# Mixer A of a two-layer diffusion trunk: rotation tables on ScalarE, and one scan over both directions

## The chip, the cores and the metric

One core of one Trainium2 chip runs the whole program in one launch. The metric is the time of one execution on the device, in microseconds (us). The comparison is between the kernel before and the kernel with the change, on the same inputs.

## The reference, cut to what matters

The reference is one inference step of a trunk of two layers over 128 context tokens and 256 latent tokens, width 1024. Layer 0 runs two mixers side by side, layer 1 two attentions; each layer ends in a gated ConvFFN. The change lies in mixer A of layer 0, a diagonal complex state space (S5) in 32 groups of 16 channels with 64 complex states each, run once forward and once backward, the two results summed:

```python
def _s5_scan(u, lam_re, lam_im, log_dt, b_re, b_im, c_re, c_im, h0_re, h0_im):
    dt = jnp.exp(log_dt)[:, None]
    mag = jnp.exp(lam_re * dt)
    ar, ai = mag * jnp.cos(lam_im * dt), mag * jnp.sin(lam_im * dt)
    ...
    _, _, hr, hi = lax.associative_scan(_cplx_combine, elems, axis=1)
    y = jnp.einsum('blgp,gcp->blgc', hr, c_re) - jnp.einsum('blgp,gcp->blgc', hi, c_im)
    return y, hr[:, -1], hi[:, -1]
...
    y_f, hr_f, hi_f = direction(uf, 0)
    y_b, hr_b, hi_b = direction(uf[:, ::-1], 1)
    y = (y_f + y_b[:, ::-1]).reshape(bsz, n, S5_WIDTH) + ...
```

Context tokens start from a zero state and their last states are outputs. Latent tokens start from given states. Mixer B is a gated DeltaNet of four heads, also in two directions, on the same input projection.

## The kernel before, in words

**Mixer A.** Four tokens are folded into one step, so a sequence has 96 steps (32 context, 64 latent) and with three extra columns for starts NCOL = 99. The 32 groups go in four octets of 8. Partitions 0 to 63 hold the 64 states of the forward direction, partitions 64 to 127 those of the backward one, in the order of the tokens. A complex recurrence is turned into two real ones by a rotation: each input is turned back by a phase that grows with the step, a real scan with the decay runs, and the result is turned forward again. For each octet:

- `s5_tables` (L436) makes the phase `ph = fh*step + fl*step` of 8 x 99 columns, rounds off whole turns twice (`sub_round`, L308: an add and subtract of a large constant, L312, then a subtraction, L313), and from it the sine `R["sn"]` and cosine `R["cs"]` on ScalarE (`sincos`, L418). VectorE does everything else: L447, L450, L451, the rounding, the fold in L422 and the decay `R["dec"]` in L455. It then makes two matrices `bt_r`, `bt_i` (L457 to L467).
- `s5_octet` (L544) multiplies the inputs `U` by `bt_r` and `bt_i` on TensorE (L559: 64 rows of inputs, 128 columns of weights, both directions in one matmul), rotates on VectorE (L563 to L565), scans the real and the imaginary part (L575 forward half, L576 backward half read from its end), rotates four products `y` (L589, L591), and sums them on TensorE into one PSUM bank `pY` of tag `sy` (L597: taps of the same step; L600: states, with both directions in the 128 rows of a matmul and an output half of 64 columns). The sum is copied out in two pieces (L602, L603), transposed twice (L606, L613) and added to the residual (L614).

`s5_taps` (L470) runs before, once for an octet, on `mm` banks.

**The order of the work.** In `layer_ab` (L1196) the setup, four `s5_taps`, `s5_tables` of octets 0 and 1 and the norm stand ahead of the projection of `u` (tags `mm` and `pj`, two banks each). Then each octet is followed in the code by the tables of the octet two ahead, a GELU and the projections of one DeltaNet head (`pj` banks; L1107, L1108, L1109 are the three matmuls of a split product, and L271 on VectorE makes the low half `wl` of a weight unit from the high half that L270 makes on ScalarE). Head 3 and the DeltaNet cores follow in a second set of PSUM banks (`ps1`, from L1236).

The order in which instructions stand on each engine is not that of the code. The class `Order` collects all instructions with their dependences, gives each a duration from fixed formulas, and lists them by longest remaining path at the time at which each could start. Its rules that matter here: a matmul on part of the columns of the array leaves TensorE free for the next instruction 20 ns later (`free[e] = s + 20`), matmuls on disjoint columns are kept together (`gangs`), a matmul that accumulates onto a region waits for the end of the one before it on that region, and a bank in rotation waits for all users of its last tile.

```python
            free[e] = s + (20 if len(held) < 4 else time)
...
                    if (w or w2) and r[0] < r2[1] and r2[0] < r[1] and r[2] < r2[3] and r2[2] < r[3]:
                        same = self.engine[j] == e and not self.dma[j]
                        self.follow(k, j, BEHIND if same and not (w2 and not w) else WAITED)
```

The engines then run their lists in order; each waits at an instruction until its data is there.

**DeltaNet core.** `state` in `gdn_core` scales a 128x128 tile `kd` by a column of `E` on VectorE (L802), four times in each of four heads, ahead of a matmul (L804).

Of the kernel before, what the change touches and what calls it, by code (L numbers as in the profile page):

```python
# [15 lines left out]
AF = mybir.ActivationFunctionType  # L16
ALU = mybir.AluOpType
# [4 lines left out]
P = 128  # L22
# [9 lines left out]
QC = 4  # L32
NCH = T // QC
NCC = NCTX // QC
NLC = NLAT // QC
NG = 32

NCOL = NCH + 3
# [3 lines left out]
MAGIC = 12582912.0  # L42
# [5 lines left out]
def _offsets(table):  # L48
# [6 lines left out]


CST_FIRST = [
    ("nidx", QC + 1), ("one", 1), ("pih", 1), ("comb", 8), ("tstep", NCOL), ("zmask", NCOL), ("ident", 128),
    ("b16", 128),
]  # L60
CST_COLS = CST_FIRST + [
# [18 lines left out]
def _consts():  # L80
    c = {}
    i = np.arange(P)
    c["ident"] = np.eye(P)
    c["ui"] = i[:, None] <= i[None, :]
    c["li"] = i[:, None] >= i[None, :]
    c["us"] = i[:, None] < i[None, :]
    c["ls"] = i[:, None] > i[None, :]
    c["nd"] = i[:, None] != i[None, :]
    for b in (16, 32, 64):
        same = (i[:, None] // b) == (i[None, :] // b)  # L90
        c[f"b{b}"] = same
        c[f"o{b}"] = ((i[:, None] // (2 * b)) == (i[None, :] // (2 * b))) & ~same
    par = np.zeros((P, 8))
    for n, b in enumerate((16, 32, 64)):
        par[:, 2 * n] = (i // b) % 2 == 0
        par[:, 2 * n + 1] = (i // b) % 2 == 1
    c["par"] = par
    c["npar"] = -par
    c["nidx"] = np.broadcast_to(np.arange(QC + 1), (P, QC + 1))
    seq = lambda n: np.concatenate([[0], np.arange(n)])  # L100
    given = lambda n: np.concatenate([[0], np.ones(n)])
    for name, f in (("tstep", seq), ("zmask", given)):
        fwd, bwd = np.concatenate([f(NCC), f(NLC), [0]]), np.concatenate([f(NLC), f(NCC), [0]])[::-1]
        c[name] = np.concatenate([np.broadcast_to(fwd, (64, NCOL)), np.broadcast_to(bwd, (64, NCOL))])
    c["ind"] = (i[:, None] % 16) == np.arange(16)[None, :]
    dinit = np.zeros((P, 2, 16))
    for p in range(P):
        dinit[p, 0, p % 16] = 1
        dinit[p, 1, 15 - p % 16] = 1
    c["dinit"] = dinit.reshape(P, 32)  # L110

    c["wm0"] = np.where(i[None, :] <= i[:, None], 0.0, -1e30)
    c["wm1"] = np.where(i[:, None] <= i[None, :], 0.0, -1e30)
    comb = np.zeros((P, 8))
    for r in range(32):
        comb[32 * (r // 8) + r % 8, r % 8] = 1
    c["comb"] = comb
    c["one"] = np.ones((P, 1))
    c["pih"] = np.full((P, 1), math.pi / 2)
    quarter = 16  # L120
    inv = 10000.0 ** (-np.arange(quarter) / quarter)
    tok = np.arange(NLAT)
    rc, rs = np.zeros((P, 2, 2, 16)), np.zeros((P, 2, 2, 16))
    for tt in range(2):
        t = tok[tt * P:(tt + 1) * P]
        for half, pos in ((0, t // 64), (1, t % 64)):
            ang = pos[:, None].astype(np.float64) * inv[None, :]
            rc[:, tt, half], rs[:, tt, half] = np.cos(ang), np.sin(ang)
    c["rcos"], c["rsin"] = rc.reshape(P, 64), rs.reshape(P, 64)
    out = np.zeros((P, NCST), np.float32)  # L130
    for name, (at, w) in CST.items():
        out[:, at:at + w] = c[name]
    return out
# [82 lines left out]
class Trunk:  # L216
# [27 lines left out]
    def t(self, pool, shape, tag, dt=F32, bufs=None):  # L244
        bufs = bufs or pool.bufs
        name = self.uid(tag)
        self.tiles[name] = (pool.name, tag, bufs, self.n)
        return pool.tile(list(shape), dt, tag=tag, name=name, bufs=bufs)
# [187 lines left out]
    def s5_tables(self, pool, tmp, o):  # L436

        nc, v, t, S = self.nc, self.nc.vector, self.t, self.S
        ident = self.c("ident")
        R = S["R"][o]  # L440
        gs = slice(8 * o, 8 * o + 8)
        sh = [P, 8, NCOL]
        step = self.c("tstep").unsqueeze(1).to_broadcast(sh)
        R["sn"] = t(pool, sh, "s5Rs", bufs=2)
        R["cs"] = t(pool, sh, "s5Rc", bufs=2)
        ph = R["cs"]
        v.tensor_mul(ph, S["fh"][:, gs].unsqueeze(2).to_broadcast(sh), step)  # L447
        self.sub_round(tmp, ph, "s5rr")
        q = t(tmp, sh, "s5rr")
        v.tensor_mul(q, S["fl"][:, gs].unsqueeze(2).to_broadcast(sh), step)  # L450
        v.tensor_add(ph, ph, q)  # L451
        self.sub_round(tmp, ph, "s5rr")
        self.sincos(R["sn"], R["cs"], ph)
        R["dec"] = t(pool, sh, "s5dec")
        v.tensor_mul(R["dec"], S["mq"][:, gs].unsqueeze(2).to_broadcast(sh),  # L455
                             self.c("zmask").unsqueeze(1).to_broadcast(sh))
        R["bt_r"] = t(pool, [P, 4, P], "s5btr", bufs=2)  # L457
        R["bt_i"] = t(pool, [P, 4, P], "s5bti", bufs=2)
        tv = t(tmp, [P, 8, 64], "s5rr")
        for key, x0, k0, x1, k1, op in (("bt_r", "br", "bar", "bi", "bsn", ALU.add),  # L460
                                        ("bt_i", "bi", "bar", "br", "bsn", ALU.subtract)):
            ba = t(tmp, [P, 8, 64], "s5tb")
            self.s5_prod(v, o, ba, S[x0], S[k0], S[x1], S[k1], op, tv)
            pt = self.bank("mod", [P, 4, P])
            for g in range(4):
                nc.tensor.transpose(pt[:, g, :], ba[:, 2 * g:2 * g + 2, :].rearrange("p g n -> p (g n)"), ident)
            nc.scalar.copy(R[key], pt)  # L467
        return R
# [75 lines left out]
    def s5_octet(self, pool, o, uT, U, R):  # L544

        nc, v, t, S = self.nc, self.nc.vector, self.t, self.S
        ident = self.c("ident")
# [6 lines left out]
        for e in range(2):  # L554
            h = slice(64 * e, 64 * e + 64)
            sr, si = self.mm(hs), self.mm(hs)
            for out, key in ((sr, "bt_r"), (si, "bt_i")):
                for q in range(4):
                    nc.tensor.matmul(out[:, q, :], R[key][h, q, :], U[h, q, :], start=True, stop=True)  # L559
            cs, sn = R["cs"][:, e::2], R["sn"][:, e::2]  # L560
            for out, x0, x1, op in ((xr[:, e::2], sr, si, ALU.add), (xi[:, e::2], si, sr, ALU.subtract)):
                tmp = t(pool, hs, "s5C", bufs=1)
                v.tensor_mul(out, x0, cs)  # L563
                v.tensor_mul(tmp, x1, sn)
                v.tensor_tensor(out, out, tmp, op)  # L565
        for x_, st in ((xr, "st_re"), (xi, "st_im")):
            nc.scalar.copy(x_[f, :, NCC + 1], self.s(st)[f, gs])
            nc.scalar.copy(x_[b, :, NCOL - 1], self.s(st)[b, gs])
        G = []
        N = 8 * NCOL  # L570
        flat = lambda ap: ap.rearrange("p g k -> p (g k)")
        for x_, name, last in ((xr, "s5gr", "last_r"), (xi, "s5gi", "last_i")):

            g_ = t(pool, [P, N + 2], name)
            v.tensor_tensor_scan(g_[f, 2:N + 2], flat(R["dec"])[f], flat(x_)[f], 0.0, ALU.mult, ALU.add)  # L575
            v.tensor_tensor_scan(g_[b, N - 1::-1], flat(R["dec"])[b, ::-1], flat(x_)[b, ::-1], 0.0, ALU.mult, ALU.add)  # L576
            g_ = g_[:, 1:N + 1].rearrange("p (g k) -> p g k", g=8)

            nc.scalar.copy(S[last][f, gs], g_[f, :, NCC + 1])
            nc.scalar.copy(S[last][b, gs], g_[b, :, 0])  # L580
            G.append(g_[:, :, 1:NCOL - 1])

        cs, sn = R["cs"][:, :, 1:NCOL - 1], R["sn"][:, :, 1:NCOL - 1]
# [7 lines left out]
                v.tensor_mul(y, x, k)  # L591
            terms.append((y, R[mat]))

        pY = self.bank("sy", [P, 4, NCH + 1])
        for q in range(4):
            for h in (f, b):
                nc.tensor.matmul(pY[h, q, :], S["tp"][h, 4 * o + q, :], U[h, q, 1:NCOL - 1], start=True, stop=False)  # L597
            for n, (y, mat) in enumerate(terms):
                for e, h in enumerate((f, b)):
                    nc.tensor.matmul(pY[h, q, :], mat[:, 2 * q + e, :], y[:, 2 * q + e, :], start=False, stop=n == 3)  # L600
        ys = t(pool, [P, 4, NCH], "gth", bufs=2)
        nc.scalar.copy(ys[:, :, 0:NCC], pY[:, :, 0:NCC])  # L602
        nc.scalar.copy(ys[:, :, NCC:], pY[:, :, NCC + 1:])  # L603
        pt = self.bank("su", [NCH, 4, P])
        for q in range(4):
            nc.tensor.transpose(pt[:, q, :], ys[:, q, :], ident)  # L606
# [102 lines left out]
    def gdn_core(self, pool, h, kT, qT, vT, zs):  # L709
# [89 lines left out]
        def state(d, c):  # L799
            col = 4 * d + h  # L800
            kd = t(pool, [P, P], "gkd", bufs=2)
            v.tensor_scalar(kd, kh[:, c, :], E[:, 1, c, col:col + 1], None, ALU.mult)  # L802
            p1 = self.bank("g4", [P, P])
            nc.tensor.matmul(p1, kd, vn[:, d, c, :], start=True, stop=True)  # L804
            if c == 0:
                nc.scalar.copy(gnew[:, d, :], p1)
            else:
                v.scalar_tensor_tensor(S1[d], S0[d], E[:, 2, c, col:col + 1], p1, ALU.mult, ALU.add)
# [1114 lines left out]
```

## Time and profile before

| what | value |
|---|---|
| median of 3 runs | 1194.18 us (1192.45 to 1199.54) |
| profiled execution, its own time | 1194.85 us |
| its span in the trace | 1193.1 us |
| TensorE busy | 1133.0 us (95%) |
| VectorE busy | 859.4 us (72%) |
| ScalarE busy | 543.7 us (46%) |
| chain that ended last | PE 85%, DVE 10%, ACT 2% |

PE is TensorE's matmuls, PEld its weight loads, DVE is VectorE, ACT is ScalarE. The span runs from the first to the last instruction; 1.75 us lie around it. Busy shares are averages over stages that differ: the start, the octets of mixer A, the DeltaNet cores, and from about 400 us on the rest.

### The profile page before, as it was taken

Reading aid. Unit: us, or ns where it says so; the run is one execution under the profiler, and the core shown is the slowest. Engines: PE = TensorE matmul, PEld = TensorE weight load, DVE = VectorE, ACT = ScalarE, POOL = GpSimd, SP = SyncE. Lnnn points to the kernel's source line nnn. Section 1 sums busy time; section 2 is a strip of 40 time slices with the busy share of each in tenths; the row PEclk is TensorE's granted clock in tenths of the full one; section 3 lists DMA queues with packets and bytes.
Section 4 is the critical chain, followed back from the end, with each engine's and each line's share of the span. In section 5 each row is a group of like instructions: output and inputs, shape, how many; then the busy total and the mean of one; then the engine's idle time right before and its main releaser. Section 6 shows DMA issues by size and latency. Waiting matters only on the chain.

```text
span 1193.1 us, 19445 instructions
## 1 busy us (share of the span) xinstructions
PE 1133.0 (95%) x7315; PEld 980.1 (82%) x7315; DVE 859.4 (72%) x2137; ACT 543.7 (46%) x1178; POOL 2.9 (0%) x15
## 2 busy tenths in 40 slices
PE   4699999999999999999999979999998999999998
PEld 1386676687558999999999968657688999999998
DVE  8997888889878768676763458886867877766432
ACT  3442333276445546555542324554535655554221
POOL 0000000000000000000000000000000000000000
PEclk8688898999999999999999989999999999999999
DMA  9233165364884333343334432311113334333541
GB/s 378 106 111 141 54 212 187 144 227 169 306 322 129 111 106 107 124 138 111 124 113 143 124 119 91 115 52 66 36 54 106 107 123 141 110 121 105 165 134 56
DMA packets 50734, 160.80 MB, mean 135 GB/s; under 512 B 8272, under 2 KB 12240, under 8 KB 50384
## 3 DMA queue, kind: packets, MB, share of 16 engines
q1 hardware_dynamic: 49200, 154.72, 38.8%
q10 hardware_dynamic: 1440, 4.85, 1.1%
q8 instruction: 57, 0.93, 0.3%
q14 instruction: 37, 0.30, 0.1%
HBM read 156.53 MB, written 3.01 MB: 134 GB/s over the span
## 4 chain that ended last, share of the span: by engine, by line
PE 85%; DVE 10%; ACT 2%; DMA 1%; issue 1%; ACTq 0%; DVEq 0%
PE mm L1107 16%; PE mm L1108 16%; PE mm L1109 16%; PE mod L992 2%; PE mm L1343 2%; PE mm L1344 2%; PE mm L1345 2%; PE sy L600 2%; PE sc L1465 1%; PE pj L1108 1%; PE pj L1107 1%; PE mm L559 1%; PE pj L1109 1%; DVE wl L271 1%; PE mod L1107 1%
## 5 line engine op out<-in xcount | busy, mean ns | idle before, releaser
L271 DVE TENSOR_TENSOR wl<-raw,wh 128x1024 fp32r<-128x1024 f32 (+2 forms) x193 | 226.9, 1194 | 111.6 <-ACT wh L270 111.2
L270 ACT CAST wh<-raw 128x1024 fp32r<-128x1024 f32 (+2 forms) x193 | 194.3, 1027 | 236.3 <-PE mm L1109 168.2
L1107 PE MATMUL mm<-ah,wl 128*128 128x386 f32 (+1 forms) x732 | 235.0, 344 | 4.1 <-DVE xt L1139 3.6
L1108 PE MATMUL mm<-al,wh 128*128 128x386 f32 (+1 forms) x732 | 233.4, 342 | 1.5 <-DVE al L1085 1.5
L1109 PE MATMUL mm<-ah,wh 128*128 128x386 f32 (+1 forms) x732 | 233.2, 341 | 0.0
L1107 PEld LDWEIGHTS mm<-ah,wl 128*128 128x128 f32 x732 | 138.6, 191 | 5.4 <-ACT wh L270 3.0
L1108 PEld LDWEIGHTS mm<-al,wh 128*128 128x128 f32 x732 | 138.6, 191 | 2.0 <-DVE al L1085 2.0
L1109 PEld LDWEIGHTS mm<-ah,wh 128*128 128x128 f32 x732 | 138.8, 191 | 0.0
L1109 PE MATMUL mm<-fgh,wh 128*128 128x384 f32 x352 | 107.2, 339 | 0.0
L1108 PE MATMUL mm<-fgl,wh 128*128 128x384 f32 x352 | 106.9, 338 | 0.0
L1107 PE MATMUL mm<-fgh,wl 128*128 128x384 f32 x352 | 106.8, 338 | 0.0
L1165 ACT ACTIVATE fz<-fz,fsh 128x128 f32<-128x128 f32 x88 | 35.5, 448 | 67.2 <-DVE fz L1162 67.2
L1107 PEld LDWEIGHTS mm<-fgh,wl 128*128 128x128 f32 x352 | 65.3, 188 | 0.0
L1108 PEld LDWEIGHTS mm<-fgl,wh 128*128 128x128 f32 x352 | 65.2, 188 | 0.0
L1109 PEld LDWEIGHTS mm<-fgh,wh 128*128 128x128 f32 x352 | 65.1, 188 | 0.0
L1139 DVE SCALAR_TENSOR_TENSOR xt<-mm,mod,xt 128x128 f32<-128x128 f32 (+1 forms) x38 | 14.0, 411 | 62.5 <-PE mm L1109 62.5
L1162 DVE TENSOR_TENSOR fz<-mm,nrb 128x384 f32<-128x384 f32 x88 | 45.8, 548 | 0.2
L1170 DVE SCALAR_TENSOR_TENSOR fy<-fz,sml,fy 128x127 f32<-128x127 f32 x88 | 36.3, 413 | 12.8 <-ACT fy L1168 12.1
L1107 PE MATMUL pj<-ah,wl 128*128 128x384 f32 x112 | 41.9, 375 | 2.2 <-DVE wl L271 2.1
L1108 PE MATMUL pj<-al,wh 128*128 128x384 f32 x112 | 42.1, 376 | 0.0
L1177 DVE SCALAR_TENSOR_TENSOR fs<-fz,fsh,fs 128x128 f32<-128x128 f32 x88 | 32.7, 412 | 12.4 <-ACT fs L1175 11.2
L1109 PE MATMUL pj<-ah,wh 128*128 128x384 f32 x112 | 41.4, 371 | 0.0
(642 smaller groups left out, 2105.7 us busy)
## 6 DMA issues: line engine op xcount, KB each, us to landing
raw<-in_ffn_up_dram SPq DMA_DIRECT2D x88, 512.0 KB, 3.4
raw<-in_w_mod_dram SPq DMA_DIRECT2D x54, 512.0 KB, 4.7
raw<-in_ffn_down_dram SPq DMA_DIRECT2D x32, 512.0 KB, 4.4
wh<-in_w_mod_dram SPq DMA_DIRECT2D x21, 512.0 KB, 6.6
wl<-in_w_mod_dram SPq DMA_DIRECT2D x21, 512.0 KB, 6.4
raw<-in_w_in_ab_dram SPq DMA_DIRECT2D x20, 512.0 KB, 3.4
raw<-in_w_in_cd_dram SPq DMA_DIRECT2D x18, 512.0 KB, 3.3
raw<-in_ffn_down_dram SPq DMA_DIRECT2D x16, 384.0 KB, 3.2
```

The costliest lines, as they stand in the source:

```text
L270: nc.scalar.copy(wh[:, :cols], raw[:, :cols])
L271: nc.vector.tensor_sub(wl[:, :cols], raw[:, :cols], wh[:, :cols].bitcast(F32))
L600: nc.tensor.matmul(pY[h, q, :], mat[:, 2 * q + e, :], y[:, 2 * q + e, :], start=False, stop=n == 3)
L992: nc.tensor.matmul(pr[32 * n:32 * n + 32], self.sc[:, k, 30 - 2 * b:62 - 2 * b], raws[n // 2][:, 512 * (n % 2):512 * (n % 2) + 512], start ...
L1107: nc.tensor.matmul(out, wl, xh, start=first, stop=False)
L1108: nc.tensor.matmul(out, wh, xl, start=False, stop=False)
L1109: nc.tensor.matmul(out, wh, xh, start=False, stop=last)
L1162: v.tensor_mul(z[i][0], ps[:, 0:T], rb)
L1165: nc.scalar.activation(pa[:, a:b], pa[:, a:b], AF.Identity, bias=sa[:, c:c + 1])
L1170: v.scalar_tensor_tensor(y[:, a + 1:b], pa[:, a:b - 1], w[:, 0:1], y[:, a + 1:b], ALU.mult, ALU.add)
L1177: v.scalar_tensor_tensor(s[:, a:b], pb[:, a:b], sb[:, c:c + 1], s[:, a:b], ALU.add, ALU.mult)
L1343: nc.tensor.matmul(ps[c], hl[k][:, ts_], wh[:, sl], start=k == 0, stop=False)
```

## The change

The backward half of every table and state is kept in reversed order, so that step 0 is its first column in both halves. The inputs of the backward half are read from their end by a matmul of their own, one scan of 128 partitions does both directions, and the products of the backward half are read from their end by the output matmuls. As one matmul can no longer sum both directions, each has its own 64 rows; sums whose rows and output columns are the same half go to `pY`, the others to a second bank `pB` from the `mm` tag, and VectorE adds the two. The tables are made of ScalarE instructions of 99 columns (one for each group) and of 792, with three VectorE instructions left. `kd` moves to ScalarE.

```diff
-        fwd, bwd = np.concatenate([f(NCC), f(NLC), [0]]), np.concatenate([f(NLC), f(NCC), [0]])[::-1]
+        fwd, bwd = np.concatenate([f(NCC), f(NLC), [0]]), np.concatenate([f(NLC), f(NCC), [0]])
...
-        ph = R["cs"]
-        v.tensor_mul(ph, S["fh"][:, gs].unsqueeze(2).to_broadcast(sh), step)
-        self.sub_round(tmp, ph, "s5rr")
-        q = t(tmp, sh, "s5rr")
-        v.tensor_mul(q, S["fl"][:, gs].unsqueeze(2).to_broadcast(sh), step)
-        v.tensor_add(ph, ph, q)
-        self.sub_round(tmp, ph, "s5rr")
-        self.sincos(R["sn"], R["cs"], ph)
+        ph, n = R["cs"], t(tmp, sh, "s5rr")
         R["dec"] = t(pool, sh, "s5dec")
-        v.tensor_mul(R["dec"], S["mq"][:, gs].unsqueeze(2).to_broadcast(sh),
-                             self.c("zmask").unsqueeze(1).to_broadcast(sh))
+        for g in range(8):
+            nc.scalar.mul(ph[:, g], self.c("tstep"), S["fh"][:, 8 * o + g:8 * o + g + 1])
+        nc.scalar.activation(n, ph, AF.Identity, bias=self.c("magic"))
+        v.scalar_tensor_tensor(ph, n, MAGIC, ph, ALU.subtract, ALU.subtract)
+        n = t(tmp, sh, "s5rr")
+        for g in range(8):
+            nc.scalar.mul(n[:, g], self.c("tstep"), S["fl"][:, 8 * o + g:8 * o + g + 1])
+        v.tensor_sub(ph, ph, n)
+        n = t(tmp, sh, "s5rr")
+        nc.scalar.activation(n, ph, AF.Identity, bias=self.c("magic"))
+        v.scalar_tensor_tensor(ph, n, MAGIC, ph, ALU.subtract, ALU.subtract)
+        nc.scalar.activation(R["sn"], ph, AF.Sin, scale=TWO_PI_DOWN)
+        nc.scalar.activation(ph, ph, AF.Abs)
+        nc.scalar.activation(ph, ph, AF.Sin, scale=-TWO_PI_DOWN, bias=self.c("pih"))
+        for g in range(8):
+            nc.scalar.mul(R["dec"][:, g], self.c("zmask"), S["mq"][:, 8 * o + g:8 * o + g + 1])
...
-                    nc.tensor.matmul(out[:, q, :], R[key][h, q, :], U[h, q, :], start=True, stop=True)
+                    nc.tensor.matmul(out[f, q, :], R[key][h, q, f], U[h, q, :], start=True, stop=True)
+                    nc.tensor.matmul(out[b, q, :], R[key][h, q, b], U[h, q, ::-1], start=True, stop=True)
...
-            v.tensor_tensor_scan(g_[f, 2:N + 2], flat(R["dec"])[f], flat(x_)[f], 0.0, ALU.mult, ALU.add)
-            v.tensor_tensor_scan(g_[b, N - 1::-1], flat(R["dec"])[b, ::-1], flat(x_)[b, ::-1], 0.0, ALU.mult, ALU.add)
+            v.tensor_tensor_scan(g_[:, 2:N + 2], flat(R["dec"]), flat(x_), 0.0, ALU.mult, ALU.add)
...
-        pY = self.bank("sy", [P, 4, NCH + 1])
+        pY, pB = self.bank("sy", [P, 4, NCH + 1]), self.mm([P, 4, NCH + 1])
...
-                for e, h in enumerate((f, b)):
-                    nc.tensor.matmul(pY[h, q, :], mat[:, 2 * q + e, :], y[:, 2 * q + e, :], start=False, stop=n == 3)
+                for e, d in ((0, 0), (1, 1), (0, 1), (1, 0)):
+                    h, r = (f, b)[e], (f, b)[d]
+                    nc.tensor.matmul((pY if d == e else pB)[h, q, :], mat[r, 2 * q + e, :],
+                                     y[r, 2 * q + e, ::-1] if d else y[r, 2 * q + e, :],
+                                     start=n == 0 and d != e, stop=n == 3)
...
-        nc.scalar.copy(ys[:, :, 0:NCC], pY[:, :, 0:NCC])
-        nc.scalar.copy(ys[:, :, NCC:], pY[:, :, NCC + 1:])
+        for to, src in ((slice(0, NCC), slice(0, NCC)), (slice(NCC, NCH), slice(NCC + 1, NCH + 1))):
+            nc.scalar.copy(ys[:, :, to], pY[:, :, src])
+            v.tensor_add(ys[:, :, to], ys[:, :, to], pB[:, :, src])
...
-            v.tensor_scalar(kd, kh[:, c, :], E[:, 1, c, col:col + 1], None, ALU.mult)
+            nc.scalar.mul(kd, kh[:, c, :], E[:, 1, c, col:col + 1])
```

## Rows read from the trace of the kernel before

**Rows 1.** Busy time by stage: stretch, length, busy us (instructions) of each engine, TensorE clock, DMA.

```profile
0.00:64.00 64.00, 36.90 (x250) 19.15 (x250) 57.82 (x168) 25.28 (x62) 2.49 (x7) 0.75 0.59 226
64.00:98.00 34.00, 33.65 (x207) 30.32 (x207) 32.86 (x68) 16.83 (x45) 0.37 (x8) 0.92 0.47 143
98.00:245.00 147.00, 140.08 (x918) 97.15 (x916) 121.15 (x221) 50.62 (x112) 0.00 (x0) 0.92 0.42 149
245.00:400.00 155.00, 151.32 (x1690) 114.53 (x1691) 127.23 (x484) 86.73 (x223) 0.00 (x0) 0.98 0.62 220
400.00:1193.00 793.00, 771.08 (x4254) 718.94 (x4252) 520.29 (x1200) 364.28 (x740) 0.00 (x0) 0.99 0.34 108
```

**Rows 2.** The same view, ten microseconds of the start: PE, PEld, DVE, ACT, POOL.

```profile
50.00:60.00 10.00, 1.70 (x8) 1.21 (x8) 9.96 (x24) 4.55 (x12) 0.00 (x0) 0.63 0.02 5
```

**Rows 3.** Timeline of TensorE there: start, length, instruction, idle before it and releaser.

```profile
58.93 0.42 PE L488 MATMUL mm<-s5Br,s5car__136_522 128*64 128x32 f32 x2 [7.43 <-DVE s5car__136_522 L434]
```

**Rows 4.** Groups of VectorE instructions by shape, 0 to 64 us: busy us, mean ns.

```profile
L313 DVE TENSOR_TENSOR s5Rc<-s5Rc,s5rr 128x792 f32<-128x792 f32 x3 | 2.9, 971 | 0.0
L447 DVE TENSOR_TENSOR s5Rc<-s5fh,cst 128x792 f32<-128x792 f32 x2 | 2.0, 977 | 0.0
L312 DVE TENSOR_SCALAR s5rr<-s5Rc 128x792 f32<-128x792 f32 x3 | 1.7, 566 | 0.0
```

**Rows 5.** Whom TensorE waited for, 64 to 245 us: total us, times, longest.

```profile
PE sy L600 <- DVE s5A L591: 3.1, 2, 2.3
PE pj L1107 <- DVE wl L271: 2.1, 2, 1.2
```

**Rows 6.** Groups of VectorE instructions by shape, 64 to 245 us, then 0 to 75 us.

```profile
L576 DVE TENSOR_TENSOR_SCAN s5gr<-s5dec,s5A 64x792 f32<-64x792 f32 x4 | 7.2, 1804 | 0.1
L575 DVE TENSOR_TENSOR_SCAN s5gr<-s5dec,s5A 64x792 f32<-64x792 f32 x4 | 7.2, 1792 | 0.0
...
L501 DVE TENSOR_TENSOR s5k<-mm,cst 128x128 f32<-128x128 f32 x4 | 1.1, 287 | 1.0 <-PE mm L499 0.8
...
L393 DVE TENSOR_TENSOR s5car<-s5mn,s5cs 64x128 f32<-64x128 f32 x2 | 0.6, 282 | 0.0
```

**Rows 7.** ScalarE: three scalings by a column (timeline), and a group with a bias column.

```profile
242.12 0.99 ACT L720 ACTIVATE ggm<-cst,gg 128x128 f32<-128x128 f32 x3
...
L423 ACT ACTIVATE s5Rc<-s5Rc,cst 128x792 f32<-128x792 f32 x4 | 3.8, 955 | 2.0 <-DVE s5Rc L422 2.0
```

**Rows 8.** Timeline of TensorE: projection matmuls in a run, then two groups of L559.

```profile
184.81 0.34 PE L1109 MATMUL pj<-ah,wh 128*128 128x384 f32 x1
184.99 0.34 PE L1107 MATMUL pj<-ah,wl 128*128 128x384 f32 x1
...
185.43 1.13 PE L559 MATMUL mm<-s5U,s5btr 64*128 64x99 f32 x8
186.40 1.05 PE L559 MATMUL mm<-s5U,s5bti 64*128 64x99 f32 x8
```

**Rows 9.** Timeline of TensorE: pairs of L600 in a run.

```profile
206.79 0.34 PE L600 MATMUL sy<-s5B,s5cai__123_471 128*64 128x97 f32 x4
206.95 0.34 PE L600 MATMUL sy<-s5A,s5car__122_470 128*64 128x97 f32 x4
```

**Rows 10.** Timeline of TensorE: a pair of L600 between projection matmuls, end of octet 3.

```profile
237.78 0.39 PE L600 MATMUL sy<-s5B,s5cai__137_523 128*64 128x97 f32 x4
238.10 0.44 PE L1109 MATMUL pj<-ah,wh 128*128 128x384 f32 x1
238.47 1.07 PE L992 MATMUL mq<-raw,msc 128*32 128x512 f32 x8
```

**Rows 11.** Timeline of TensorE: matmuls on quarters of the array in two banks, first to next.

```profile
284.49 0.27 PE L952 MATMUL g<-cst,gTc 64*64 64x64 f32 x1
...
285.16 0.38 PE L765 MATMUL g<-gqT,gkhT 128*128 128x128 f32 x1
```

**Rows 12.** One line of the DeltaNet core: minimum, median, maximum ns, first and last start.

```profile
L802 DVE TENSOR_SCALAR gkd<-gkh,gE x16: 277/280/288, 253.5 to 388.3; 128x128 f32<-128x128 f32 x16
```

More of the change, by code (lines that the diff above doesn't have):

```diff
@@ L57 @@
 CST_FIRST = [
-    ("nidx", QC + 1), ("one", 1), ("pih", 1), ("comb", 8), ("tstep", NCOL), ("zmask", NCOL), ("ident", 128),
+    ("nidx", QC + 1), ("one", 1), ("pih", 1), ("magic", 1), ("comb", 8), ("tstep", NCOL), ("zmask", NCOL), ("ident", 128),
     ("b16", 128),
@@ L118, in _consts @@
     c["one"] = np.ones((P, 1))
+    c["magic"] = np.full((P, 1), MAGIC)
     c["pih"] = np.full((P, 1), math.pi / 2)
@@ L442, in s5_tables @@
         sh = [P, 8, NCOL]
-        step = self.c("tstep").unsqueeze(1).to_broadcast(sh)
         R["sn"] = t(pool, sh, "s5Rs", bufs=2)
         R["cs"] = t(pool, sh, "s5Rc", bufs=2)
-        ph = R["cs"]
-        v.tensor_mul(ph, S["fh"][:, gs].unsqueeze(2).to_broadcast(sh), step)
-        self.sub_round(tmp, ph, "s5rr")
-        q = t(tmp, sh, "s5rr")
-        v.tensor_mul(q, S["fl"][:, gs].unsqueeze(2).to_broadcast(sh), step)
-        v.tensor_add(ph, ph, q)
-        self.sub_round(tmp, ph, "s5rr")
-        self.sincos(R["sn"], R["cs"], ph)
-        R["dec"] = t(pool, sh, "s5dec")
-        v.tensor_mul(R["dec"], S["mq"][:, gs].unsqueeze(2).to_broadcast(sh),
-                             self.c("zmask").unsqueeze(1).to_broadcast(sh))
+        ph, n = R["cs"], t(tmp, sh, "s5rr")
+        R["dec"] = t(pool, sh, "s5dec")
+        for g in range(8):
[14 more added lines that the diff above has]
+            nc.scalar.mul(R["dec"][:, g], self.c("zmask"), S["mq"][:, 8 * o + g:8 * o + g + 1])
         R["bt_r"] = t(pool, [P, 4, P], "s5btr", bufs=2)
@@ L567, in s5_octet @@
             nc.scalar.copy(x_[f, :, NCC + 1], self.s(st)[f, gs])
-            nc.scalar.copy(x_[b, :, NCOL - 1], self.s(st)[b, gs])
+            nc.scalar.copy(x_[b, :, 0], self.s(st)[b, gs])
         G = []
@@ L574, in s5_octet @@
             g_ = t(pool, [P, N + 2], name)
-            v.tensor_tensor_scan(g_[f, 2:N + 2], flat(R["dec"])[f], flat(x_)[f], 0.0, ALU.mult, ALU.add)
-            v.tensor_tensor_scan(g_[b, N - 1::-1], flat(R["dec"])[b, ::-1], flat(x_)[b, ::-1], 0.0, ALU.mult, ALU.add)
+            v.tensor_tensor_scan(g_[:, 2:N + 2], flat(R["dec"]), flat(x_), 0.0, ALU.mult, ALU.add)
             g_ = g_[:, 1:N + 1].rearrange("p (g k) -> p g k", g=8)
             nc.scalar.copy(S[last][f, gs], g_[f, :, NCC + 1])
-            nc.scalar.copy(S[last][b, gs], g_[b, :, 0])
+            nc.scalar.copy(S[last][b, gs], g_[b, :, NCOL - 1])
             G.append(g_[:, :, 1:NCOL - 1])
```

## The prediction

> **What bounds the kernel now.** I read the busy times by stage first [rows 1], because the page's 95% for TensorE is an average. From 400 us on TensorE is busy for 771 of 793 us with matmuls that the change doesn't touch, so a gain can only come from the first 400 us and is then carried to the end unchanged. In the first 64 us TensorE is busy for 36.9 us at 0.75 of its clock while VectorE is busy for 57.8. Between 50 and 60 us this is plain: VectorE 9.96 of 10 us, TensorE 1.70 [rows 2], and TensorE's timeline shows 7.43 us of idle time ahead of the taps of octet 3, ended by VectorE [rows 3]. So the start is bound by VectorE. From 64 to 245 us, where the octets and three heads run, TensorE is busy for 174 of 181 us at 0.92 of its clock and VectorE for 154; here TensorE sets the pace, with waits for VectorE of 3.1 us on the rotated products and 2.1 us on low halves of weights [rows 5]. From 245 to 400 us TensorE is busy for 151 of 155 us. ScalarE is busy for 25.3 of the first 64 us and 67 of the next 181: it has room.
>
> **The change part by part, against the profiled execution (1194.85 us, 0.67 above the median of 1194.18).**
>
> *Tables in the start.* In the first 64 us VectorE runs twelve 792-column instructions of tables 0 and 1: three of L313, two each of L447, L450 and L451 (the last two cost what L447 costs) and three of L312 [rows 4]: 9 x 0.97 + 3 x 0.57 = 10.4 us. The new tables need three of 0.97 us each, 5.8 us for both. If all six still stand ahead of 64 us, VectorE is freed by 4.6 us; if only three do, by 7.5. As TensorE waits for VectorE here [rows 3], this comes through, up to those 7.43 us. ScalarE takes on, per octet, 24 scalings by a column. Three of 128 columns take 0.99 us [rows 7]; 24 of these would take 7.9 us, and 99 columns cost no more. Two roundings and an absolute value, at most 0.96 us each [rows 7], add 2.9. That is 10.8 us per octet, 21.6 for two, on top of 25.3 busy in 64 [rows 1]: it fits, but ScalarE works in order, and the high halves of weights, the norm's high parts and the copies of taps stand behind scalings. That can eat the whole gain, so the bounds are 0 and -7.5; I take -5, near the lower of the two sums. Next late in the start is the norm on VectorE, then TensorE itself.
>
> *Scans and tables in the octets.* A scan over 64 partitions takes 1.80 us, forward and from its end alike [rows 6]. A VectorE product of 128 columns takes 0.28 us on 64 partitions and 0.29 on 128 [rows 6], so a scan of 128 should cost the same 1.80 and each octet saves 3.6 us. The two later tables save 10.4 - 5.8 us and, with L422 and the decay (four more of 0.97), 3.9: 8.5 us. The two additions per octet read PSUM: 0.29 us for 128 columns [rows 6], at most double for 256, 0.9 in all. VectorE so loses 14.4 + 8.5 - 3.6 = 19 of its 154 us. Off the path, this is worth nothing; on it are the 5.2 us of waits [rows 5]. The 3.1 should go, as the scans stand right ahead of those products; of the 2.1 little. I take -3.5, bounds 0 and -5.2.
>
> *Input matmuls (L559).* Four of 128 columns take 0.97 us, start to start [rows 8]; 64 of them 15.5. Each becomes a pair on disjoint column halves. Pairs of L600 start every 0.16 us in a run [rows 9], which would make 64 pairs 10.2 us; a pair that stands alone takes 0.32 [rows 10], 20.5 us. No row shows TensorE reading a moving operand from its end; VectorE does so at no cost [rows 6], which is the nearest. At half rate a pair would take 0.32 in a run. Bounds -5 and +5; I take -2, since the planner finds no cause to part these pairs.
>
> *Output matmuls (L600).* Today a pair accumulates onto the region of the pair before it, so the planner lets a projection matmul in between. That is dear: pair to projection 0.32 us, projection to the next 0.37 [rows 10], against 0.16 for a pair in a run [rows 9] and 0.18 for a projection matmul in a run [rows 8]. By the timeline 52 of the 64 pairs stand alone: 52 x (0.32 + 0.19) + 12 x 0.16 = 28.4 us. After, each product has two pairs, one for `pY` and one for `pB`, that don't depend on each other. While the first holds TensorE, the other is ready, then the next product's first. With the longer paths they stand in runs. Runs on quarters of the array exist: twelve matmuls of 64 columns in two banks take 0.67 us [rows 11], 0.87 ns per column, where the pairs of [rows 9] make 0.16 / (2 x 97) = 0.82. By rows, then, two run at a time, and a product costs 0.32. 64 x 0.32 plus 16 runs x 0.35 for going in and out is 26.1 us: -2. Bounds: with each second pair alone as well, 64 x 0.51 more, +31; with four at a time, 64 x 0.16 + 5.6 = 15.8, -12.
>
> The Trainium skill ("TensorE: Matmul & The Clock Gate", Part 3) says that matmuls on tiles with rows and columns of their own run at once, some 4 ns apart. By that rule the two pairs would cost 0.16 together and this term would be -12, as in rival 1. The trace agrees for column halves and not for quarters.
>
> *The rest.* `pB` takes one of two `mm` banks until the additions end, so the next octet's `bt_i` matmuls queue behind. In this trace only octet 2's first half runs beside its forerunner's output; cost 0 to +4, I take +0.5 with the additions ahead of the last transposes, which the following modulation matmul covers. `kd`: 16 x 0.28 us leave VectorE [rows 12], at most 0.4 each come to ScalarE (87 of 155 busy); 0, bounds -1 and +2. TensorE's clock: 0.92 over 181 us [rows 1] is 14 us lost at the lower of its two levels, in stretches after waits; with fewer waits I take -1.5, bounds -4 and +2.
>
> Sum: -5 - 3.5 - 2 - 2 + 0.5 + 0 - 1.5 = -13.5, which is 1181.3 against the profiled execution; I say 1181.
>
> **The rivals.**
>
> 1. *Everything better*: quarters run four at a time and the start gains 7. 1181 - 10 - 2 = 1169. For it: the run of quarters in [rows 11] includes its drain. Against: 0.87 ns.
>
> 2. *ScalarE takes the place of VectorE in the start.* The 48 small scalings stand ahead of what VectorE and TensorE wait for, the start gains nothing and some waits stay: 1181 + 5 + 2.5 = 1188.5. For: strict order, 10.8 us per table in one chain. Against: ScalarE is idle for 38.7 of 64 us, and the first octet asks for its table only when the projection of `u` is done.
>
> The Trainium skill ("ScalarE: Activation LUTs", Rules for kernel authors) tells authors to leave multiplications and additions to VectorE. By that rule this rival is the likelier. Here a scaling of 128 columns takes 0.28 us on VectorE [rows 12] and 0.33 on ScalarE [rows 7], a small difference while ScalarE idles.
>
> 3. *Reading from the end costs TensorE half its rate.* Every pair contains such a read. An input pair takes 0.16 us more, 10 in all; a product of two plain and two slow matmuls, two at a time, 0.48 in place of 0.32, 10 in all: 1181 + 10 + 10 = 1201. The change would then not do what it says.
>
> 4. *Slower: the second pairs stand alone.* If projection matmuls have the longer path than the `pB` pairs, each such pair costs 0.51 us, less the 0.16 it had in my sum. It needs 39 of 64 to undo the gain (13.5 / 0.35); with all 64, and the next octets' inputs late by 4 us because `pB` stays full, 1181 + 22 + 4 = 1207; with a start that gains nothing, 1212. For: 52 of 64 stand alone today. Against: the projection's remaining path falls with each matmul while the waiting pair's doesn't, so the pair soon leads.
>
> **How the numbers follow.** Forecast 0.46 (1174 to 1188); rival 1 0.15 (1164 to 1174); rival 2 0.17 (1184 to 1193); rival 3 0.08 (1195 to 1204); rival 4 0.14 (1204 to 1215). The range is 1165 to 1204: it leaves out rival 4 and the lower edge of rival 1. A measurement of this kernel tells about 1%, 12 us, from no change, so faster means under 1182.3: six tenths of the forecast and rival 1, 0.28 + 0.15 with 0.05 for a quicker rival 2 or 3: 0.48. Slower means over 1206: 0.12. Within: 0.40.
>
> **What would show it.** In the changed kernel's profile: scans of 128x792 at 1.80 us, two per octet; the idle time ahead of L488 near 2 us in place of 7.43, and the first projection matmul some 5 us earlier; pairs of the output in runs, with 0.16 or 0.32 per product; waits on L591 gone. A scan of 128 partitions over 1.80, small scalings at over 0.33 us each in a row, output pairs between projection matmuls, or a run of L559 pairs at 0.32 would make the prediction wrong.

## The result, and the profile after

The changed kernel takes 1176.52 us (median of 4 runs, 1175.78 to 1179.21) against 1194.66 us for the kernel before, measured beside it: a ratio of 0.985, 95% interval 0.9832 to 0.9868, so 18 us or 1.5% faster. The forecast was 1181 in a range of 1165 to 1204. The profiled execution took 1175.78 us, its span 1174.0 against 1193.1.

Busy time by stage, after (columns as in [rows 1]):

```profile
0.00:64.00 64.00, 42.65 (x266) 24.19 (x267) 54.80 (x163) 38.39 (x101) 2.49 (x7) 0.76 0.62 235
64.00:98.00 34.00, 31.83 (x251) 27.05 (x250) 29.75 (x69) 19.22 (x53) 0.37 (x8) 1.00 0.52 157
98.00:245.00 147.00, 139.41 (x1355) 103.92 (x1355) 115.80 (x248) 79.64 (x194) 0.00 (x0) 0.97 0.49 168
245.00:400.00 155.00, 149.70 (x1667) 111.32 (x1667) 125.33 (x464) 93.08 (x246) 0.00 (x0) 1.00 0.61 210
400.00:1174.00 774.00, 754.58 (x4165) 703.76 (x4164) 505.52 (x1158) 352.17 (x711) 0.00 (x0) 0.99 0.33 108
...
50.00:60.00 10.00, 7.04 (x58) 5.75 (x56) 9.61 (x23) 9.38 (x27) 0.00 (x0) 0.57 0.21 63
```

Against [rows 1]: ScalarE has 13.1 us more to do in the first 64 us, VectorE 3.0 less, and TensorE does 5.8 us more in them. From 64 to 245 us VectorE's work falls from 154.0 to 145.6 us, although all stages have moved forward and the last of these microseconds already belong to the DeltaNet cores. TensorE's granted clock rises from 0.92 to 1.00 and to 0.97. What is lost at the lower of its two levels (1.2 and 2.4 GHz) falls from 0.08 x 34 + 0.08 x 147 = 14.5 us to 0.03 x 147 = 4.4. After 400 us TensorE is as full as before (755 of 774 us, 771 of 793 in [rows 1]); the stage is shorter only because it starts further into the program.

TensorE's timeline at the start, with the idle time ahead of an instruction and what ended it:

```profile
58.67 0.69 PE L1119 MATMUL mm<-ah,wl 128*128 128x384 f32 x1 [1.53 <-DVE s5k L508]
...
85.64 0.35 PE L605 MATMUL sy<-s5U,s5tp 64*64 64x97 f32 x2 [1.03 <-DMA s5tp<-s5kd]
...
86.64 0.35 PE L605 MATMUL sy<-s5U,s5tp 64*64 64x97 f32 x2 [0.28 <-DMA s5tp<-s5kd]
```

The idle time of 7.43 us [rows 3] is gone, and the first projection matmul starts at 58.67 us in place of 64.35. The two lower rows are new: TensorE now reaches the first tap matmul of an octet before the taps `s5tp` have come back from memory.

VectorE's scans, by line (minimum, median, maximum ns; first and last start):

```profile
L583 DVE TENSOR_TENSOR_SCAN s5gr<-s5dec,s5A x4: 1797/1800/1809, 92.0 to 199.3; 128x792 f32<-128x792 f32 x4
...
L583 DVE TENSOR_TENSOR_SCAN s5gi<-s5dec,s5B x4: 1780/1782/1800, 93.8 to 201.0; 128x792 f32<-128x792 f32 x4
```

128 partitions cost what 64 did in [rows 6]. These rows also give the place of the gain. The first scan starts at 92.0 us (before: 91.7), the last at 201.0 (before: 222.2). Head 3's first projection matmul, which ends the octets on TensorE, starts at 221.90 (before: 241.49): 19.6 us earlier, and the span is shorter by 19.1. By these times the gain lies between the first scan and the end of the octets, and the 5.7 us of the start can no longer be seen at the first scan; in their place TensorE has done 21 more projection matmuls by 92 us (67 on `pj` against 46).

Whom TensorE waited for, 58 to 400 us:

```profile
PE pj L1119 <- DVE wl L272: 2.3, 3, 1.2
PE su L618 <- ACT gE L688: 1.7, 1, 1.7
...
PE sy L605 <- DMA s5tp<-s5kd: 1.3, 2, 1.0
...
PE sy L609 <- DVE s5A L598: 0.8, 2, 0.6
```

L598 is the L591 of [rows 5]: 3.1 us have become 0.8, and no total in the list exceeds 2.3 us.

The input pairs and the output pairs in TensorE's timeline (each matmul shows as two records, so in the output rows x2 is half a pair):

```profile
81.26 0.25 PE L566 MATMUL mm<-s5U,s5btr 64*64 64x99 f32 x1
81.27 0.24 PE L567 MATMUL mm<-s5U,s5btr 64*64 64x99 f32 x1
81.35 0.24 PE L566 MATMUL mm<-s5U,s5btr 64*64 64x99 f32 x1
81.35 0.24 PE L567 MATMUL mm<-s5U,s5btr 64*64 64x99 f32 x1
...
100.86 0.25 PE L609 MATMUL mm<-s5A,s5car__94_366 64*64 64x97 f32 x2
100.88 0.25 PE L609 MATMUL sy<-s5B,s5cai__95_367 64*64 64x97 f32 x2
100.94 0.25 PE L609 MATMUL mm<-s5B,s5cai__95_367 64*64 64x97 f32 x2
100.96 0.25 PE L609 MATMUL sy<-s5B,s5cai__95_367 64*64 64x97 f32 x2
```

Half an input pair comes every 0.085 us, so a pair every 0.17, and the matmul that reads `U` from its end (L567) lasts as long as the other. In the output run `sy` advances by half a pair every 0.08 us, and `mm` does so at the same time: a whole product, two pairs on four quarters of the array, takes 0.16 us, as one pair did in [rows 9]. The prediction had 0.32. The Trainium skill ("TensorE: Matmul & The Clock Gate", Part 3) says that tiles with rows and columns of their own run at once; this trace agrees, for quarters too.

### The profile page after: what moved, and what is told of

It reads as the page before. It is cut to its first block, busy times and chain, and to the rows that moved or that the text cites. A ratio compares the mean times of both kernels' runs of the same rounds, so it can differ in the third digit from the quotient of the medians.

```text
span 1174.0 us, 20291 instructions
## 1 busy us (share of the span) xinstructions
PE 1118.2 (95%) x7699; PEld 970.2 (83%) x7699; DVE 831.2 (71%) x2097; ACT 582.5 (50%) x1301; POOL 2.9 (0%) x15
## 4 chain that ended last, share of the span: by engine, by line
PE 85%; DVE 8%; DMA 2%; ACT 2%; issue 1%; ACTq 0%; DVEq 0%; SPq 0%
PE mm L1120 16%; PE mm L1121 16%; PE mm L1119 16%; PE mod L1004 3%; PE mm L1355 2%; PE mm L1356 2%; PE mm L1357 2%; PE sc L1477 1%; DVE wl L272 1%; PE mod L1119 1%; PE pj L1121 1%; PE mod L1120 1%; PE mq L1004 1%; PE pj L1120 1%; PE pj L1119 1%
## 5 line engine op out<-in xcount | busy, mean ns | idle before, releaser
L272 DVE TENSOR_TENSOR wl<-raw,wh 128x1024 fp32r<-128x1024 f32 (+2 forms) x193 | 227.0, 1194 | 118.1 <-ACT wh L271 117.8
L1119 PE MATMUL pj<-ah,wl 128*128 128x384 f32 x112 | 39.4, 353 | 2.3 <-DVE wl L272 2.3
L1189 DVE SCALAR_TENSOR_TENSOR fs<-fz,fsh,fs 128x128 f32<-128x128 f32 x88 | 32.7, 413 | 12.4 <-ACT fs L1187 11.2
L1355 PE MATMUL mm<-wh,al 128*128 128x512 f32 (+1 forms) x120 | 38.8, 396 | 2.0 <-DVE al L1074 2.0
```

The costliest lines, as they stand in the source:

```text
L272: nc.vector.tensor_sub(wl[:, :cols], raw[:, :cols], wh[:, :cols].bitcast(F32))
L1119: nc.tensor.matmul(out, wl, xh, start=first, stop=False)
L1189: v.scalar_tensor_tensor(s[:, a:b], pb[:, a:b], sb[:, c:c + 1], s[:, a:b], ALU.add, ALU.mult)
L1355: nc.tensor.matmul(ps[c], hl[k][:, ts_], wh[:, sl], start=k == 0, stop=False)
```

## The experiments

Each kernel is named with its edit. Ratios are to the kernel before, measured on the same chip between the runs; "over" and "under" the changed kernel compares with 1176.5 us. The kernel before took 1194.8 us beside experiments 1 to 4, 1195.3 beside 5 to 8 and 1195.9, on another chip, beside 9 to 12, so differences of a microsecond are read from the ratios.

**1. The tables alone.** The kernel before with the new body of `s5_tables` and nothing else.

```
-        v.tensor_mul(ph, S["fh"][:, gs].unsqueeze(2).to_broadcast(sh), step)
-        self.sub_round(tmp, ph, "s5rr")
...
+        for g in range(8):
+            nc.scalar.mul(ph[:, g], self.c("tstep"), S["fh"][:, 8 * o + g:8 * o + g + 1])
...
```

Expected: 

> The kernel before with the new making of the rotation tables alone (scalings, rounding sums and absolute value on ScalarE; the backward half still in its old order). Theory: the start's gain is the tables' and is carried to the end: the first projection matmul 5 to 6 us earlier than at 64.35, and the time 1187 to 1190 us. Rival: the tables of octets 2 and 3 were on the path too, through VectorE, and the clock rises with them: 1180 to 1184 us. Second rival: the earlier start is lost again at the octets, which then wait for their products: 1193 to 1196 us.

Measured: 1190.53 us, ratio 0.9964 (0.9937 to 0.999), 4.3 us faster. The first projection matmul starts at 58.82 us. The first theory was right about the place, and the time lies just above its range; of 5.5 us some 4 arrive.

**2. All but the tables.** The changed kernel with the old body of `s5_tables`.

Expected: 

> The changed kernel with the tables made on VectorE as before. Theory: the parts add up, so that this loses the 5.7 us of the start and 0 to 3 us of the octets: 1182 to 1186 us, first projection matmul at 64 us. Rival: the start was paid twice, and the octets take it back when it is gone: 1177 to 1179 us.

Measured: 1178.03 us, ratio 0.986 (0.9846 to 0.9875). This is the rival's time, and the parts don't add up: on top of the rest the tables are worth some 1.5 us, no more than the intervals leave open. The first projection matmul comes at 69.11 us, 10.4 later than in the changed kernel, the first scan at 96.4 (4.4 later), the first matmul of head 3 at 222.95 (1.05 later). The octets take back nearly all of a late start.

**3. Two chains of output pairs.** The kernel before, with its pairs of 128 rows sent in turn to two banks.

```
+        pY, pB = self.bank("sy", [P, 4, NCH + 1]), self.mm([P, 4, NCH + 1])
...
+                    nc.tensor.matmul((pB if n % 2 else pY)[h, q, :], mat[:, 2 * q + e, :], y[:, 2 * q + e, :],
+                                     start=n == 1, stop=n > 1)
...
+            v.tensor_add(ys[:, :, to], ys[:, :, to], pB[:, :, src])
```

Expected: 

> The kernel before with one edit: each octet's four rotated products go in turn into two banks, sy and mm, and are added as in the changed kernel. Tiles stay 128 rows by 64 columns, the scans stay four of 64 partitions, nothing is read from its end. Theory: a pair stood alone because it had to wait for the pair before it in the same bank; with two chains the pairs stand in runs, the output falls from about 0.5 to 0.16 us a pair for most of the 52 lone pairs, and the time is 1182 to 1188 us. Rival: pairs stand alone because VectorE gives the products late, one by one, behind its scans; then this gains nothing and the additions cost a little: 1193 to 1197 us.

Measured: 1197.11 us, ratio 1.002 (0.9993 to 1.0048); its ten times fall into two groups, five at 1190 to 1194 us with a mean clock of 0.964 to 0.968 and five at 1200 to 1203 us with 0.956 to 0.959. No gain. Yet the edit does what the theory asked: in the order of TensorE's starts 46 stretches of exactly one output pair become 10. Whom TensorE then waits for, 60 to 245 us:

```profile
PE sy L600 <- DVE s5A L591: 7.6, 3, 2.9
PE mm L488 <- DVE s5car__136_522 L434: 4.4, 1, 4.4
```

The wait on the rotated products has grown from 3.1 us [rows 5] to 7.6. TensorE is done sooner and then waits for VectorE. Lone pairs cost TensorE time, as the rows behind experiment 6 show, but the theory that removing them shortens the kernel by itself falls.

**4. Scans in halves.** The changed kernel with `for h in (f, b)` around the scan, so that VectorE has 14.4 us more in the octets.

Expected: 

> The changed kernel with each scan of 128 partitions cut into two of 64, both forward: 3.6 us more of VectorE per octet, 14.4 in all. Theory: TensorE sets the pace in the octets and the scans are mostly hidden: 1177 to 1181 us. Rival: the halved scans are the main gain of the octets, and their time comes back in full or with a lower clock: 1185 to 1192 us.

Measured: 1189.78 us, ratio 0.9968 (0.995 to 0.9987), 13.3 us over the changed kernel: the rival. With experiment 3 I read this as: the scans are the bulk. The next two runs test it.

**5 and 6. One scan, without and with two chains.** The kernel before with one scan of 128 partitions from the front, first alone, then with the edit of experiment 3.

```
-            v.tensor_tensor_scan(g_[f, 2:N + 2], flat(R["dec"])[f], flat(x_)[f], 0.0, ALU.mult, ALU.add)
-            v.tensor_tensor_scan(g_[b, N - 1::-1], flat(R["dec"])[b, ::-1], flat(x_)[b, ::-1], 0.0, ALU.mult, ALU.add)
+            v.tensor_tensor_scan(g_[:, 2:N + 2], flat(R["dec"]), flat(x_), 0.0, ALU.mult, ALU.add)
...
```

Expected of the first: 

> The kernel before with one scan of 128 partitions from the front in place of two of 64; it leaves out the backward half's own order, everything else stands. Theory, from the runs so far: in the octets TensorE is late after each scan, so the 14.4 us of VectorE are on the path nearly in full even with the old output, with fewer waits on the rotated products and a higher clock: 1179 to 1186 us. Rival: scans and output pairs in runs are two halves of one gain, and the scan alone is held up by the long row of lone output pairs: 1188 to 1194 us.

Expected of the second: 

> The kernel before with one scan of 128 partitions (the backward half's own order left out) and the rotated products in two chains of banks sy and mm. Theory: once VectorE no longer comes late, pairs in runs are worth something on TensorE as well: 4 to 8 us under the kernel with the one scan alone. Rival: TensorE's time in the octets is never the limit, and the two chains are worth nothing, within 2 us of it, or cost the additions: up to 4 us over it.

Measured: 1192.08 us, ratio 0.9968 (0.9945 to 0.9992), and 1177.19 us, ratio 0.9853 (0.9831 to 0.9875). My theory of the scans falls here, and its rival holds; the second theory had the direction, but its 4 to 8 us became 15:

| ratio to before | output in one chain | in two chains |
|---|---|---|
| two scans of 64 | 1 | 1.002 |
| one scan of 128 | 0.9968 | 0.9853 |

Each alone is worth at most 4 us, both together 17.6, as much as the whole change (0.985). With the one scan alone 56 such stretches of a lone pair remain (11 with both), and VectorE waits, 64 to 225 us:

```profile
DVE s5A L563 <- PE mm L559: 6.1, 6, 2.3
...
DVE s5A L563 <- PE sy L599: 3.3, 2, 1.9
```

In the second row the rotation of the next octet waits until the last lone pairs have read the buffer `s5A`. The kernel before has that row too, with 3.7 us; with both edits it is gone from the list, in which 4.0 us of waits of the additions for the output are new. Whether more buffers for `s5A` would do as well was not tried.

TensorE's own time shows how the two edits need each other. From the start to head 3's first projection matmul (length, busy time, clock; what follows takes 949 to 952 us in all five): the kernel before, two chains alone, one scan alone, both, and the changed kernel:

```profile
0.00:241.49 241.49, 207.24 (x1354) 0.87 0.47 166
0.00:241.33 241.33, 195.74 (x1360) 0.87 0.48 170
0.00:235.41 235.41, 199.58 (x1354) 0.91 0.47 171
0.00:225.57 225.57, 188.43 (x1359) 0.90 0.51 183
0.00:221.90 221.90, 191.37 (x1737) 0.92 0.53 184
```

Two chains save TensorE 11.5 us with two scans and 11.2 with one. With two scans its idle time (length less busy time) grows by 11.3 us, from 34.3 to 45.6, and nothing is left; with one scan it grows by 1.3, from 35.8 to 37.1, and the saving reaches the end. One reservation stays: the planner gives each of these kernels an order of its own, and what share of the 17.6 us the order has is not shown.

The last cell is also the control for the rest of the output's edit: it has no quarters and reads nothing from the end, and with the old tables it takes what experiment 2 takes (0.986). Quarters and reversed reads make one scan of both directions possible, and cost nothing that can be measured.

**7. Tables mixed.** The changed kernel, with the old table code for octets 2 and 3 (`if o < 2:` around the new). It was made for a row of the changed kernel. ScalarE's timeline there:

```profile
175.29 1.28 ACT L688 ACT_TABLE_LOAD   x1
...
177.07 0.92 ACT L463 ACTIVATE s5dec<-cst,s5mq 128x99 f32<-128x99 f32 x3
177.89 0.62 ACT L621 COPY s5um<-su 96x256 f32<-96x256 f32 x2
178.41 1.46 ACT L463 ACTIVATE s5dec<-cst,s5mq 128x99 f32<-128x99 f32 x5
```

A copy for which TensorE waits (L621) stands among scalings of a later table.

Expected: 

> The changed kernel with the tables of octets 0 and 1 made by ScalarE and those of octets 2 and 3 by VectorE as before. Theory: with all tables on VectorE the first scan came 4.4 us later but the last one only 1.7, so ScalarE's scalings hold the octets up by some 3 us; the mixture keeps the start and loses this: 1172 to 1175 us. Rival: VectorE's 8.5 us more in the octets come through as the scans' did: 1178 to 1184 us.

Measured: 1182.37 us, ratio 0.9896 (0.9865 to 0.9927): not faster than the changed kernel but slower, as the rival had it. Its price, though, isn't VectorE's 8.5 us, since experiment 2 pays those as well and takes 1178. Its profiled execution, the slowest of its four, reaches the first scan at 96.7 us in place of 92.0 (see experiment 10), and between 225 and 245 us its clock is 0.66. What causes the latter stays open.

**8 and 9. `kd` back on VectorE**, first with a free order, then with the order held: the planner counts the 16 steps as ScalarE's, so that TensorE's order is that of the changed kernel.

```
-            nc.scalar.mul(kd, kh[:, c, :], E[:, 1, c, col:col + 1])
+            v.tensor_scalar(kd, kh[:, c, :], E[:, 1, c, col:col + 1], None, ALU.mult)
```

Expected of the first: 

> The changed kernel with kd made on VectorE as before. Prediction's term: 0, bounds -1 and +2, so 1174 to 1178 us. Rival: the 16 steps stand in a chain with VectorE and the time rises by their 4.5 us, or by part of it: 1179 to 1181 us.

Expected of the second: 

> The changed kernel with kd made on VectorE, but the planner still counts it as ScalarE's, so that TensorE's order and all else stand as in the changed kernel. Theory: kd itself is worth about nothing, and the 4.4 us of the free version came from another order of the first 100 us (its first scan starts at 98.1 us, in the changed kernel at 92.0): 1175 to 1178 us. Rival: the 16 steps themselves stand in VectorE's chain: 1179 to 1182 us.

Measured: 1180.91 us, ratio 0.9889 (0.987 to 0.9909), and 1180.17 us, ratio 0.9877 (0.986 to 0.9895). The times agree with the rival in both cases. The line of `kd`, in the changed kernel and then in the one with the order held, doesn't:

```profile
L814 ACT ACTIVATE gkd<-gkh,gE x16: 386/403/415, 233.0 to 370.5; 128x128 f32<-128x128 f32 x16
```

```profile
L814 DVE TENSOR_SCALAR gkd<-gkh,gE x16: 247/280/286, 235.7 to 374.1; 128x128 f32<-128x128 f32 x16
```

At the first of the 16 steps 2.7 us of the 3.9 between the two spans (1174.0 and 1177.9) are lost already; from the first to the last it is 138.4 us in place of 137.5. So the steps themselves account for 0.9 us at most in this pair of executions, and most of the rest arose ahead of them.

**10. Plain reads.** The changed kernel without `::-1` in both matmuls. The order on every engine is the same, so this is also a second sample of the changed kernel's order.

Expected: 

> The changed kernel with both reads from the end (input and output matmuls) made forward; it leaves out the turning of the backward half's order, and the order of all instructions is that of the changed kernel. Theory: a moving operand read from its end costs TensorE nothing: 1174 to 1179 us, pairs at the same spacing. Rival of the prediction: it costs half the rate; then this gains up to 20 us where they lie on the path: 1157 to 1170 us.

Measured: 1179.38 us (1172.71 to 1182.6), ratio 0.9861 (0.9822 to 0.99). The median lies just above the 1179 expected, far from the rival's 1157 to 1170, and its L567 lasts 246 ns with plain reads and 245 in the changed kernel (medians). Reading from the end costs nothing that these runs show.

Its profiled execution, with a span of 1179.2 us, also shows where it and the kernel of experiment 9 lost their time. Plain reads, 84 to 98 us (TensorE's clock is the third number from the end), with the timeline's row:

```profile
84.00:90.00 6.00, 3.18 (x13) 1.77 (x9) 2.36 (x4) 1.58 (x3) 0.00 (x0) 0.76 0.83 220
90.00:98.00 8.00, 8.00 (x56) 7.31 (x59) 3.85 (x7) 1.80 (x8) 0.00 (x0) 0.54 0.14 51
```

```profile
86.86 0.35 PE L605 MATMUL sy<-s5U,s5tp 64*64 64x97 f32 x2 [2.37 <-DMA s5tp<-s5kd]
```

The same in the changed kernel:

```profile
84.00:90.00 6.00, 4.69 (x52) 3.47 (x49) 3.79 (x7) 1.85 (x5) 0.00 (x0) 1.00 0.88 278
90.00:98.00 8.00, 7.42 (x60) 5.61 (x59) 7.91 (x9) 5.32 (x20) 0.00 (x0) 1.00 0.36 136
```

And with `kd` on VectorE, order held:

```profile
84.00:90.00 6.00, 3.62 (x30) 2.32 (x27) 2.68 (x4) 1.58 (x3) 0.00 (x0) 0.93 0.98 256
90.00:98.00 8.00, 8.00 (x52) 6.51 (x49) 5.21 (x8) 2.14 (x10) 0.00 (x0) 0.62 0.07 28
```

With the same order TensorE waited for the first two transfers of taps 1.3 us (1.03 and 0.28) in one execution and 2.8 (2.37 and 0.45) in another, and 2.4 with `kd` on VectorE. After the longer waits it went through the next 8 us at 0.54 and 0.62 and came to the first scan at 97.4 and 96.0 us in place of 92.0. The profiled execution of the changed kernel is one in which this didn't happen; why the transfer came later in the others is not shown. Kernels with an order of their own show the same. The tables alone (experiment 1), and then experiment 2, which reaches the taps later and doesn't wait for them, 90 to 98 us:

```profile
90.00:98.00 8.00, 8.00 (x37) 0.58 0.02 9
```

```profile
90.00:98.00 8.00, 8.00 (x78) 1.00 0.46 136
```

Experiment 1 waited 1.8 us for taps, and experiments 7 and 8 2.9 each, with 0.63 and 0.57 behind it. That is one place where the tables' gain in the start is lost again. So times of single variants between 1176 and 1182 are hardly told apart by four runs each, and that holds for `kd` and for experiment 7 too.

**11. Scans in halves, order held.** Experiment 4, planned as if the two scans took the time of one.

Expected: 

> The changed kernel with each scan cut into two of 64 partitions, but planned as if the two took the time of one, so that TensorE's order stays nearly that of the changed kernel. Theory: the scans' time itself is on the path: 1186 to 1192 us, with waits on the rotated products. Rival: the 13 us of the free version came in large part from another order: 1178 to 1183 us.

Measured: 1208.57 us, ratio 1.0111 (1.0084 to 1.0138): 32 us over the changed kernel (31 by the ratios) for 14.4 us of VectorE, past what either theory had. Clock and TensorE's waits, 98 to 245 us and 58 to 400 us:

```profile
98.00:245.00 147.00, 127.05 (x1196) 91.55 (x1194) 111.36 (x197) 64.53 (x163) 0.00 (x0) 0.86 0.39 140
```

```profile
PE pj L1119 <- DVE wl L272: 6.3, 2, 5.1
PE sy L609 <- DVE s5A L598: 6.2, 2, 4.3
PE sy L609 <- DVE s5B L596: 3.7, 1, 3.7
```

TensorE is busy for 12.4 us less of these 147 than in the changed kernel, and 0.11 x 147 = 16 us more of the stage's clock is lost. The waits for VectorE behind the scans cost twice: themselves, and the stretch at the lower level that follows. Waits of 4.31, 5.11 and 3.72 us end at 103.41, 155.74 and 226.11 us, and TensorE's clock is 0.50 from 106 to 110, from 158 to 162 and from 230 to 246 us. The planner's freedom in experiment 4 had saved 17 us of that by the ratios.

**12. Taps on GpSimd.** The changed kernel with `self.s5_prod(nc.gpsimd if o else v, o, R["ca_i"], ...)`, an attempt at something faster still.

Expected: 

> The changed kernel with the three 512-column products of the taps' second half moved from VectorE to GpSimd for octets 1 to 3, nine in all. Theory: VectorE still ends the start, so that 6.2 us less of it brings the first projection matmul forward by 2 to 5 us, of which as little is left at the end as of the tables' gain, 1 to 2 us: 1173 to 1176 us. Rival: GpSimd is too slow for the taps of octets 1 to 3, TensorE waits for them, and the planner's order of the first 100 us is worse: 1178 to 1185 us.

Measured: 1182.59 us, ratio 0.9893 (0.987 to 0.9917). The rival holds. The first projection matmul comes at 59.84 us, not earlier; a 512-column product or sum on GpSimd took 1.05 to 2.04 us, against 0.68 on VectorE. No version beats the changed kernel.

## Why the prediction was right or wrong

The time was 4.5 us under the forecast, inside the likeliest case's own range of 1174 to 1188. The sum came out nearly right with terms that did not, in part by luck.

- *Tables in the start, -5.* The trace shows -5.7 at the place named: the idle time ahead of octet 3's taps is gone, ScalarE had the room, and rival 2 fell for the start. At the end the tables bring 4.3 us alone and 1.5 on top of the rest. "Next late in the start is the norm, then TensorE" missed the taps' transfer, which appears in no wait of the kernel before and behind which part of the early start is lost again (experiment 10).
- *Scans and tables in the octets, -3.5, bounds 0 and -5.2.* This step failed. VectorE's saving was sized rightly (3.6 us an octet, 1.80 us a scan), but its worth was bounded by the waits on VectorE that the profile listed. Undoing the scans alone costs 13.3 us, and 32 with the order held. The sentence behind it, that from 64 to 245 us TensorE sets the pace, was half the truth: both engines were nearly full and took turns, and relief of TensorE alone became idle time (the five rows behind experiment 6). Waits were not where the gain came from: to head 3's first matmul the changed kernel has 3.7 us less idle time and 15.9 us less busy time, where the prediction put 8.5 of its 13.5 us into waits.
- *Output matmuls, -2.* A product costs 0.16 us in a run, the bound of -12 and the mechanism of rival 1. The 0.87 ns per column of [rows 11] that spoke against it comes from a short run with its drain, which the prediction itself put in rival 1's favour. But TensorE's time alone was worth nothing: two chains by themselves gave 1.002. Two counts were off as well: by order of starts 48 pairs stood apart from others, not 52, and the bound of +31 counts the second pair twice, at 0.16 and at 0.51 us; with the 0.35 of rival 4 it is +20.
- *Input matmuls, -2.* Pairs stand in runs at 0.17 us as costed; rival 3 falls (experiment 10).
- *TensorE's clock, -1.5, bounds -4 and +2.* Failed too: the loss in the octets fell from 14.5 to 4.4 us. I counted waits and clock as separate small terms, where the stretch after a wait can cost more than the wait (experiments 10 and 11). What the rise is worth by itself is not shown: the kernel with one scan and two chains has 0.90 to head 3's first matmul, the changed one 0.92, and they take the same time.
- *`kd`, 0.* At most 0.9 us by the trace, inside its bounds; the 3 us by the ratio in experiment 9 fall mostly ahead of the steps. *Additions and `pB`, +0.5*: not isolated; they are part of the control in experiment 6, which costs nothing visible.
- *Rival 4* (second pairs alone) hardly occurred: the two banks' pairs stand together in the rows at 100.86 us, and over all octets 10 stretches of exactly one pair are left, where it needed 39.

The Trainium skill ("ScalarE: Activation LUTs", Rules for kernel authors) would leave the tables' multiplications on VectorE. Experiment 1 speaks against that here by 4.3 us, experiment 2, on top of the rest, by some 1.5. A scaling of 99 columns took 0.37 us on ScalarE by itself and 0.31 in a row of three (0.92 us), within the 0.33 that the prediction allowed.

The sum was close because two errors met. I added terms that only work as a product: as independent terms, scan and output should have been worth their sum in the table of experiments 5 and 6, at most 4 us; together they gave 17.6, where my terms for them (-3.5, which holds the later tables too, -2, +0.5 and -1.5 for the clock) make -6.5. Against that, the tables' -5 became some 1.5 on top of the rest, and for the -2 of the input matmuls nothing is left. That the two nearly cancel was luck.

## What to carry to other kernels

Where two engines are both nearly full and feed each other, list the relief of each and ask whether it survives without the other; test the 2 x 2, since either edit alone may look worthless. The listed waits on an engine are no upper bound for what freeing it is worth: look as well at the stretch at the lower clock behind each wait, and at the other engine's time that can't reach the end without it. When a stage is brought forward, look for the transfer that used to land just in time.

## What the runs showed that I had not expected

- 14.4 us of VectorE on the path cost 32 us with the order held, about half of it at TensorE's lower clock.
- The same order of instructions ran the stretch from 90 to 98 us at a clock of 1.00 or 0.54, after waits of 1.3 or 2.8 us in all for the same two transfers. A version that issues the tap matmuls behind the rotated products, so that no one waits there, was not tried.
- Four 64x64 matmuls on quarters of the array, in two banks, take the 0.16 us of one pair on halves, accumulating, and with one operand read from its end.
